# Down products accumulated in PSUM as chains, weight loads tied to matmuls, input rows read once, in a one-core decoder step

## The chip, the cores and the metric

The kernel runs on one core of one Trainium2 chip. The core has TensorE (PE; its weight loads are listed apart as PEld), VectorE (DVE), ScalarE (ACT), GpSimd (POOL) and SyncE (SP), which here only issues DMA transfers. PSUM, the matmuls' output memory, has 8 banks. The metric is the device time of one execution in microseconds (us).

## The reference

One layer of a decoder over 1024 prompt rows and 8 x 8 sample rows, 1088 tokens in all, in float32. The part that the change touches is its end:

```python
mixed = jax.nn.sigmoid(g_a) * branch_a + jax.nn.sigmoid(g_b) * branch_b
h = x + jnp.einsum('btd,de->bte', mixed, w_o)
z = jnp.einsum('btd,df->btf', rms_norm(h, ln2), w_up)
return h + jnp.einsum('btf,fd->btd', jnp.square(jax.nn.relu(z)), w_down)
```

The model width is 1024 and z is 4096 wide. Ahead of it come the input projection, a causal pooling branch and three groups of dilated attention, which make `mixed`, and updated caches are part of the output.

## The kernel before

Everything is transposed: tokens lie along the free axis, channels on the 128 partitions. The 1088 tokens are ordered in four residues of 272 (`Q`); a half (`H`) is two of these, 544 tokens. Each float32 operand of a matmul is split into a high and a low part by one ScalarE copy and one VectorE subtraction (`split`, `put`, lines 113, 1382), and each product is three matmuls (high x high, high x low, low x high).

TensorE's order is the order of the program text. The instructions of the other engines, and of SP's transfer queue, are put in order by a planner that simulates the program; each engine and queue then works strictly in its order. `behind_pe` (line 172) makes an instruction wait for a given matmul; without an argument it takes the last matmul traced by the helpers that keep `last_mm`.

**w_o (lines 1335 to 1355).** For each half `j` of the tokens and each of four weight panels `d`, the panel is read in four 256 KB pieces (three raw buffers, L120) and split (L114, L115). The input rows `xr` of two channel blocks, all 1088 tokens, are read in each of the eight rounds (L1339), into two buffers. VectorE adds them to the product (L1348), giving h: `y[j][kk]`, which is stored (L1349) and squared for the second norm. The norm of half 0 is worked out during half 1, that of half 1 (`norm_sums(1)`, `norm_spread(1)`) after the first two Up products; from it `make_versions` (line 1407) makes the differences of quarters of the normed input.

**Up and Down** are each done with seven products of quarter blocks in place of eight (Strassen's scheme in Winograd's form), in 16 groups. A step is one product for one group: 24 matmuls. `step` puts preparation, matmuls, what follows (`post`), and a load in a list, and `run` (line 1467) emits it: at step n first the loads of steps up to n + 8, then the preparations up to n + 2, then the matmuls, the post, and one of the `later` actions. Preparation splits a weight into one of five places; `raw_tile` has two buffers.

*Up* (`group`, line 1517): P1 is copied out of its PSUM tile by ScalarE (L1532) and P2 is then accumulated onto the same tile. For the first five groups (`FIRST`) P1 and P2 come first, ten steps, while the other operands are made; their results go through the single buffers e1 and e2 (`park`) to memory and are read back (`back`, L1554). The quarters of weights for these ten steps are `raw_uf` (L1497). Afterwards come P5, P6, P7, P3, P4 for these groups, then all seven for the others. Each group's squared results and their sums are stored as seven blocks `z_d` (L1515).

*Down* (`down_stage`, line 1690) has seven stages, in the order P2, P4, P1, P5, P6, P7, P3; a stage is 16 steps, which accumulate into four PSUM tiles of two banks each, all of PSUM. A step loads 256 KB of w_down and 272 KB of z into a half of a raw buffer, or the weight into one of 32 `kept` tiles that later stages use. At a stage's end `post_down` (line 1659) reads the four tiles out: by VectorE, adding onto h rows `hs` or onto `running` (P2, P4, P6), by ScalarE into `running` or `parked` (P1, P5, P7), and by VectorE into the output rows (P3). 24 adds onto `hs` and 8 output row halves are spread over the following steps, one action a step. The h rows are read back in the first stage (L1705).

GpSimd issues 44 transfers that move the caches from input to output (line 1763). Each waits for one of a list of marks, ScalarE splits all along the program.

## Time and profile before

| | us |
|---|---|
| median of 3 runs (1495.24 to 1497.19) | 1496.16 |
| profiled execution | 1495.8 |
| its span, first to last instruction | 1494.0 |
| TensorE busy in it | 1442.5 |
| mean granted TensorE clock | 0.986 |

A row of the timeline gives start, length, engine, line of the kernel, operation, output<-inputs, shape and count; in brackets, how long the engine had stood and what ended that. A row of waits gives total time, times, and the longest. A row of a stretch gives its length, the busy time (and count) of PE, PEld, DVE, ACT and POOL, the granted clock of TensorE as a share of full speed, the mean busy share of the 16 DMA engines, and GB/s. Tile names are the program's: ph is a w_o product, pz an Up product, pd a Down product, places and apart hold split weights.

### The profile page before, as it was taken

To read this page: it belongs to the slowest core of one execution; us is meant where nothing else is said; L and a number is where in the kernel's file an instruction comes from. 1 tells how busy PE (TensorE), PEld (TensorE's weight loads), DVE (VectorE), ACT (ScalarE), POOL (GpSimd) and SP (SyncE) were. 2 spreads that over 40 slices of the span, in tenths; PEclk is the share of its full clock that TensorE was granted. 3 is DMA by queue.
4 is the path that set the end of the run, shared out by engine and by line. 5 is a ranking of instruction groups with operands and counts; after the bars stand their busy time and mean duration, and the time that the engine had idled before them with its cause. 6 is when DMAs were issued, how large, how long until landed. Compare 5 with 4: busy or idle time off the path is not lost. (4 is left out here: it accounts for less than half of the span.)

```text
span 1494.0 us, 28199 instructions
## 1 busy us (share of the span) xinstructions
PE 1442.5 (97%) x10765; PEld 1386.0 (93%) x10765; DVE 899.7 (60%) x1704; ACT 702.0 (47%) x1884; POOL 204.4 (14%) x245
## 2 busy tenths in 40 slices
PE   9999999999999999998998989999999799999988
PEld 8988877888899999998997989999999799999888
DVE  7665674866755444244578766665655345784865
ACT  8566755877533232123435434544454344443342
POOL 1711255556300000010000000000000000000000
PEclk9999999999999999999998999999999899999999
DMA  6312888553545432379757766565668944655664
GB/s 202 110 46 78 229 202 202 169 134 94 148 129 181 136 126 97 113 216 320 263 188 226 249 222 211 186 193 197 208 205 322 352 158 151 224 189 185 204 219 160
DMA packets 164276, 277.91 MB, mean 186 GB/s; under 512 B 32615, under 2 KB 86189, under 8 KB 162414
## 3 DMA queue, kind: packets, MB, share of 16 engines
q1 hardware_dynamic: 158030, 225.79, 47.5%
q0 software_dynamic: 6112, 50.33, 10.6%
q8 instruction: 84, 1.38, 0.4%
q14 instruction: 50, 0.41, 0.1%
HBM read 215.74 MB, written 103.98 MB: 214 GB/s over the span
## 5 line engine op out<-in xcount | busy, mean ns | idle before, releaser
L1741 PE MATMUL pd<-places 128*128 128x272 f32 x2688 | 340.8, 289 | 16.5 <-ACT places L1384 8.4
L1741 PEld LDWEIGHTS pd<-places 128*128 128x128 f32 x2688 | 338.3, 190 | 19.0 <-ACT places L1384 11.1
L1763 POOL DMA_DIRECT2D out_kv_sample_dram<-in_cache_kv_dram x44 | 21.9, 497 | 944.7 <-ACT places L1384 494.9
L1384 ACT ACTIVATE places<-raw_d 128x544 fp32r<-128x544 f32 (+1 forms) x160 | 99.1, 641 | 98.7 <-PE pd L1741 26.0
L1385 DVE TENSOR_TENSOR places<-raw_d,places 128x544 fp32r<-128x544 f32 (+1 forms) x160 | 109.7, 711 | 32.5 <-ACT places L1384 32.2
L1454 PE MATMUL pz<-act,places 128*128 128x272 f32 x912 | 119.5, 289 | 2.8 <-ACT e L1532 2.8
L1454 PEld LDWEIGHTS pz<-act,places 128*128 128x128 f32 x912 | 116.5, 188 | 3.3 <-ACT e L1532 3.2
L184 PE MATMUL ph<-act,places 128*128 128x272 f32 x768 | 99.5, 292 | 5.1 <-ACT places L114 5.1
L184 PEld LDWEIGHTS ph<-act,places 128*128 128x128 f32 x768 | 98.5, 191 | 5.6 <-ACT places L114 5.6
L184 PE MATMUL pga<-act,places 128*128 128x384 f32 (+1 forms) x576 | 100.2, 332 | 0.2 <-ACT places L114 0.2
L184 PE MATMUL pgb<-act,places 128*128 128x384 f32 (+1 forms) x576 | 97.9, 327 | 0.0
L184 PEld LDWEIGHTS pga<-act,places 128*128 128x128 f32 x576 | 96.3, 190 | 1.2 <-issue 0.6
L184 PEld LDWEIGHTS pgb<-act,places 128*128 128x128 f32 x576 | 95.4, 188 | 0.0
L1454 PE MATMUL pz<-act,apart 128*128 128x272 f32 x624 | 85.9, 297 | 6.6 <-ACT e L1532 6.6
L1454 PEld LDWEIGHTS pz<-act,apart 128*128 128x128 f32 x624 | 83.5, 196 | 7.1 <-ACT e L1532 7.0
L1384 ACT ACTIVATE places<-kept 128x512 fp32r<-128x512 f32 x64 | 40.5, 632 | 104.5 <-PE pd L1741 87.4
L1385 DVE TENSOR_TENSOR places<-kept,places 128x512 fp32r<-128x512 f32 x64 | 44.1, 689 | 65.1 <-ACT places L1384 65.0
L600 POOL TENSOR_TENSOR mr<-ms,mhalf 128x4 f32<-128x4 f32 (+2 forms) x39 | 51.9, 1332 | 106.6 <-DVE ms L599 106.4
L1454 PE MATMUL pz<-places 128*128 128x272 f32 x432 | 58.9, 295 | 4.1 <-DVE t L1591 4.1
L184 PE MATMUL pqk<-places,act 128*128 128x512 f32 x240 | 61.0, 403 | 1.0 <-ACT qk L605 1.0
L1454 PEld LDWEIGHTS pz<-places 128*128 128x128 f32 x432 | 57.4, 196 | 4.3 <-issue 4.3
L184 PEld LDWEIGHTS pqk<-places,act 128*128 128x128 f32 x240 | 44.6, 192 | 11.1 <-ACT qk L605 1.2
(382 smaller groups left out, 2657.0 us busy)
## 6 DMA issues: line engine op xcount, KB each, us to landing
out_kv_sample_dram<-in_cache_kv_dram POOLq DMA_DIRECT2D x36, 960.0 KB, 6.2
raw_d<-z_d SPq DMA_DIRECT2D x112, 272.0 KB
z_d<-t SPq DMA_DIRECT2D x86, 272.0 KB
raw_u<-in_w_up_dram SPq DMA_DIRECT2D x64, 256.0 KB
raw_d<-in_w_down_dram SPq DMA_DIRECT2D x64, 256.0 KB
raw_qkv<-in_w_in_dram SPq DMA_DIRECT2D x36, 256.0 KB
xr<-in_xT_dram SPq DMA_DIRECT2D x8, 1088.0 KB
pck<-in_cache_kv_dram SPq DMA_DIRECT2D x32, 256.0 KB
```

What stands on the lines that cost most here:

```text
L184: last_mm[0] = t_.matmul(out, lhs(a, k), rhs(b, k), start=(j == 0), stop=(j == len(terms) - 1))
L600: g_.tensor_tensor(r[:n, :H], ms[:n, :H], mhalf[:n, :H], op=ALU.pow)
L1384: ins = s_.activation(view(t[:, 0]), src, AF.Copy)
L1385: v_.tensor_tensor(view(t[:, 1]), src, view(t[:, 0]).bitcast(F32), op=ALU.subtract)
L1454: t_.matmul(x[:, c, :Q], A[:, a, k * P:(k + 1) * P], Bv(b, k, c), start=(first and n == 0), stop=(n == len(terms) - 1), skip_group_check=n ...
L1741: t_.matmul(q["x"][t][:, c, :Q], A[:, a, t * P:(t + 1) * P], Z[:, b, c * Q:(c + 1) * Q], start=(f == 0 and n == 0), stop=(f == NG - 1 and ...
L1763: ins = g_.dma_start(d, a)
```

## The change

Six things are changed.

- Input rows: `xr` is read only for half 0. ScalarE copies the rows of half 1 into `y[1]`, and in half 1 VectorE adds the product onto them.
- Loads: a step's load is now emitted `lead` steps ahead of it (7 in Up, 6 for the first ten steps, 4 for the first panel of an early group and in Down, never below step 0) and by `behind_pe` waits for the last matmul before that point. The reloads of an early group move from the load to the preparation of P5.
- The first groups' results: e1 and e2 serve every third group, the others use the two buffers t1, t2 each.
- Down's order is P2, P1, P6, P7, P4, P5, P3. P6, P7 and P4 accumulate in PSUM onto P1, and P3 onto P5; P2, P1 and P5 start anew. The weight sums change with it: one block is now read once where it was read twice, another three times instead of once, 16 loads more in all. The h rows are read in the third stage.
- After each stage but the last, ScalarE copies the four tiles into `park_a` or `park_b`; 16 VectorE adds and 8 row halves follow.
- The cache transfers get no mark in Down's first two stages and twice as many in P5.

```diff
@@ -1335,8 +1335,9 @@
     for j in range(2):
         for d in range(4):
             wt = by_k(panel(i["w_o"][d], f"o{j}{d}"))
-            xr = rr(hq_p, [P, 2, TOK], F32, name=f"xr{j}{d}", tag="xr", bufs=2)
-            dma(xr, i["xT"][:, 2 * d:2 * d + 2])
+            if j == 0:
+                xr = rr(hq_p, [P, 2, TOK], F32, name=f"xr{d}", tag="xr", bufs=2)
+                dma(xr, i["xT"][:, 2 * d:2 * d + 2])
             for m in range(2):
                 kk = 2 * d + m
                 po = xtile(f"ph{kk}_{j}")
@@ -1345,7 +1346,11 @@
                     gemm(po[:, c, :Q], KD, lambda s, k: wt[:, s, k, m * P:(m + 1) * P], lambda s, k: act[s][k][:, cs])
                     if todo:
                         todo.pop(0)()
-                v_.tensor_tensor(two(y[j][kk]), xs_of(po), by_token(xr[:, m, :], j), op=ALU.add)
+                if j == 0:
+                    v_.tensor_tensor(two(y[0][kk]), xs_of(po), by_token(xr[:, m, :], 0), op=ALU.add)
+                    s_.copy(two(y[1][kk]), by_token(xr[:, m, :], 1))
+                else:
+                    v_.tensor_tensor(two(y[1][kk]), xs_of(po), two(y[1][kk]), op=ALU.add)
                 dma_st(h_d[kk][:, half(j)], y[j][kk])
                 if kk == 0:
                     s_.activation(sqa[j], y[j][kk], AF.Square)
@@ -1366,7 +1371,7 @@
...
-                t_.matmul(x[:, c, :Q], A[:, a, k * P:(k + 1) * P], Bv(b, k, c),
-                          start=(first and n == 0), stop=(n == len(terms) - 1), skip_group_check=not first)
...
+                last_mm[0] = t_.matmul(x[:, c, :Q], A[:, a, k * P:(k + 1) * P], Bv(b, k, c),
+                                       start=(first and n == 0), stop=(n == len(terms) - 1), skip_group_check=not first)
...
+    def step(prep, mm, post, load=None, lead=7):
+        if load:
+            loads.setdefault(max(0, len(queue) - lead), []).append(load)
+        queue.append((prep, mm, post))
...
+    def run(ahead=3):
+        n_prep = 0
...
-            while n_load < min(len(queue), n + load_ahead):
-                if queue[n_load][0]:
-                    queue[n_load][0]()
-                n_load += 1
+            for load in loads.get(n, ()):
+                load()
...
     def load_panel(f):
         raws[f] = raw_tile(f"u{f}")
         for a in range(0, 2048, 512):
-            dma(raws[f][:, a:a + 512], i["w_up"][f][:, a:a + 512])
+            behind_pe(dma(raws[f][:, a:a + 512], i["w_up"][f][:, a:a + 512]))
...
     def load_first(f):
         if f % 2 == 0:
             raws["first", f // 2] = raw_tile(f"uf{f}")
         for a in range(2):
-            dma(first_quarter(f, a).rearrange("p (k n) -> p k n", k=4),
-                i["w_up"][f].rearrange("p (k n) -> p k n", k=8)[:, 4 * a:4 * a + 4, :P])
+            behind_pe(dma(first_quarter(f, a).rearrange("p (k n) -> p k n", k=4),
+                          i["w_up"][f].rearrange("p (k n) -> p k n", k=8)[:, 4 * a:4 * a + 4, :P]))
...
-    def park(n, name):
-        return rr(up, [P, H], F32, name=f"e{n}_{name}", tag=f"e{n}", bufs=1)
+    def park(n, f):
+        if f % 3:
+            return temp(n, f"e{f}")
+        return rr(up, [P, H], F32, name=f"e{n}_{f}", tag=f"e{n}", bufs=1)
...
             step(lambda: weights(0, 0), lambda A: products(xt(), A, B["11"], True), first_post,
-                 (lambda: load_first(f)) if early else (lambda: load_panel(f)))
+                 (lambda: load_first(f)) if early else (lambda: load_panel(f)), 6 if early else 7)
...
         def back():
-            load_panel(f)
             for n, src in ((1, p_d[f]), (2, z_d[f, :, 0, :])):
                 firsts[f][n - 1] = temp(n, f"again{f}")
                 dma(firsts[f][n - 1], src)
@@ -1563,8 +1569,12 @@
                 q["x5"] = q["x"]
                 q["s5"] = temp(4, f)
                 s_.copy(two(q["s5"]), xs_of(q["x"]))
-            step(lambda: summed(1, quarter(f, 1, 0), quarter(f, 1, 1), ALU.add),
-                 lambda A: products(xt(), A, B["T1"], True), post, back if early else None)
+            def prep():
+                if early:
+                    back()
+                return summed(1, quarter(f, 1, 0), quarter(f, 1, 1), ALU.add)
+            step(prep, lambda A: products(xt(), A, B["T1"], True), post,
+                 (lambda: load_panel(f)) if early else None, 7 if f else 4)
...
         for t in range(4):
             x = xs_of(xs[t])
-            v, w = parked[:, t], running[:, t]
-            if p in (2, 4):
-                kt = t if p == 2 else 4 + t
-                v_.tensor_tensor(two(hs[kt][:, half(0)]), two(hs[kt][:, half(0)]), x, op=ALU.add)
+            a, b = park_a[:, t], park_b[:, t]
+            if p == 2:
+                s_.copy(two(a), x)
             if p == 1:
-                s_.copy(two(w), x)
-                later.append(adds(t, 0, w))
+                s_.copy(two(b), x)
+                later.append(lambda a=a, b=b: v_.tensor_tensor(a, a, b, op=ALU.add))
+            if p == 6:
+                s_.copy(two(b), x)
+                later.extend((adds(t, 0, a), adds(t, 1, b)))
+            if p == 7:
+                s_.copy(two(a), x)
+                later.append(adds(4 + t, 1, a))
+            if p == 4:
+                s_.copy(two(b), x)
+                new_row(4 + t)
+                later.append(lambda t=t, b=b: row_half(4 + t, 0, two(b)))
             if p == 5:
-                s_.copy(two(v), x)
-                later.extend((adds(t, 1, v), adds(4 + t, 1, v)))
-            if p == 6:
-                v_.tensor_tensor(two(w), two(w), x, op=ALU.add)
-                later.extend((adds(4 + t, 0, w), adds(t, 1, w), adds(4 + t, 1, w)))
-            if p == 7:
-                s_.copy(two(v), x)
-                new_row(4 + t)
-                later.append(lambda t=t, v=v: row_half(4 + t, 0, two(v)))
-                later.append(lambda t=t, v=v: (row_half(4 + t, 1, two(v)), row_done(4 + t)))
+                s_.copy(two(a), x)
+                later.append(lambda t=t, a=a: (row_half(4 + t, 1, two(a)), row_done(4 + t)))
             if p == 3:
                 row_half(t, 1, x)
                 row_done(t)
-        if p == 7:
+        if p == 5:
             for t in range(4):
                 later.append(lambda t=t: (new_row(t), s_.copy(by_token(rows[t], 0), two(hs[t][:, half(0)]))))
...
         def load(f):
-            if p == 2 and f >= KD:
-                kt = f - KD
-                hs[kt] = op.tile([P, TOK], F32, name=f"hs{kt}")
-                dma(hs[kt], h_d[kt])
+            if p == 6 and f % 2 == 0:
+                hs[f // 2] = op.tile([P, TOK], F32, name=f"hs{f // 2}")
+                behind_pe(dma(hs[f // 2], h_d[f // 2]))
             if f % 2 == 0:
                 q[f] = raw_tile(f"d{p}_{f}")
             w, z = parts(f)
-            if p == 4:
-                dma(kept[1, f], of(f, 1, 1))
-            elif p == 1:
-                dma(kept[2, f], of(f, 0, 0))
-            elif p != 6:
-                dma(w, of(f, *((1, 0) if p in (5, 7) else (0, 1))))
-            dma(z, z_d[f, :, ZI[p], :])
+            block = {2: (0, 1), 1: (1, 0), 7: (1, 1), 4: (1, 1), 3: (0, 1)}.get(p)
+            if block:
+                behind_pe(dma(w, of(f, *block)))
+            behind_pe(dma(z, z_d[f, :, ZI[p], :]))
+            if p == 1:
+                behind_pe(dma(kept[1, f], of(f, 0, 0)))
+            n = f + {2: -4, 1: 12}.get(p, NG)
+            if 0 <= n < NG:
+                behind_pe(dma(kept[2, n], of(n, 1, 1)))
...
         def prep(f):
             w, z = parts(f)
-            if p in (4, 1):
-                w = kept[1 if p == 4 else 2, f]
-            elif p in (5, 6):
-                k1 = kept[1, f]
-                if p == 5:
-                    v_.tensor_tensor(k1, w, k1, op=ALU.add)
-                else:
-                    v_.tensor_tensor(k1, k1, kept[2, f], op=ALU.subtract)
+            k1, k2 = kept.get((2, f)), kept.get((1, f))
+            if p == 1:
+                v_.tensor_tensor(k1, w, k1, op=ALU.add)
+                w = k2
+            elif p == 6:
+                v_.tensor_tensor(k2, k1, k2, op=ALU.subtract)
+                w = k2
+            elif p == 5:
                 w = k1
-            elif p == 7:
-                v_.tensor_tensor(w, kept[2, f], w, op=ALU.subtract)
-            elif p == 3:
-                v_.tensor_tensor(w, w, kept[1, f], op=ALU.subtract)
+            elif p in (7, 3):
+                v_.tensor_tensor(w, w, k2, op=ALU.subtract)
             return put_down(w, z)
         def mm(f, AZ):
             A, Z = AZ
-            if f == 0:
-                q["x"] = [xtile(f"pd{p}_{t}") for t in range(4)]
+            fresh = p in (2, 1, 5)
+            if f == 0 and fresh:
+                chain[:] = [xtile(f"pd{p}_{t}") for t in range(4)]
+            q["x"] = chain
             for t in range(4):
                 for c in range(2):
                     for n, (a, b) in enumerate(PASSES):
-                        t_.matmul(q["x"][t][:, c, :Q], A[:, a, t * P:(t + 1) * P], Z[:, b, c * Q:(c + 1) * Q],
-                                  start=(f == 0 and n == 0), stop=(f == NG - 1 and n == 2))
+                        last_mm[0] = t_.matmul(chain[t][:, c, :Q], A[:, a, t * P:(t + 1) * P], Z[:, b, c * Q:(c + 1) * Q],
+                                               start=(fresh and f == 0 and n == 0), stop=(f == NG - 1 and n == 2),
+                                               skip_group_check=not fresh)
         for f in range(NG):
             step(lambda f=f: prep(f), lambda AZ, f=f: mm(f, AZ),
-                 (lambda: post_down(p, q["x"])) if f == NG - 1 else (lambda: None), lambda f=f: load(f))
-
-    for p in (2, 4, 1, 5, 6, 7, 3):
+                 (lambda: post_down(p, q["x"])) if f == NG - 1 else (lambda: None), lambda f=f: load(f), 4)
+
+    chain = []
+    for p in (2, 1, 6, 7, 4, 5, 3):
         down_stage(p)
...
     n_up = 7 * NG
     late = [t for t in throttle[13:-8] for _ in range(4)] + [t for t in throttle[-8:] for _ in range(2)]
-    late += marks_f[:n_up] + marks_f[n_up + 24:-20:2]
+    down = [marks_f[n_up + 32 * n:n_up + 32 * n + 32:2] for n in range(7)]
+    late += marks_f[:n_up] + [m for n in (2, 3, 4, 5, 5, 6) for m in down[n][:16 - 10 * (n == 6)]]
```

22 lines of the change are left out of this document (9 added, 13 removed).

## The prediction

> **What bounds the kernel now.** I read the page first (engine shares), then who TensorE waited for, then TensorE's timeline around each pause, then the loads and the queue that caused it. Of the page:
> ```profile
> span 1494.0 us, 28199 instructions
> PE 1442.5 (97%) x10765; PEld 1386.0 (93%) x10765; DVE 899.7 (60%) x1704; ACT 702.0 (47%) x1884; POOL 204.4 (14%) x245
> raw_d<-z_d SPq DMA_DIRECT2D x112, 272.0 KB
> raw_d<-in_w_down_dram SPq DMA_DIRECT2D x64, 256.0 KB
> ```
> TensorE is busy 97%, and the change removes no matmul. So all that can be won is pauses, and the slow clock behind them. The waits of TensorE from 665 to 1130 us (w_o and the Up products), and in Down, which follows:
> ```profile
> PE pz L1454 <- ACT e L1532: 9.3, 4, 4.7
> PE ph L184 <- ACT places L114: 5.1, 1, 5.1
> PE pz L1454 <- DVE t L1591: 4.1, 1, 4.1
> ```
> ```profile
> L1741 PE MATMUL pd<-places 128*128 128x272 f32 x2688 | 340.8, 289 | 16.5 <-ACT places L1384 8.4
> ```
> That is 18.5 us before Down (columns: total, times, longest) and, by the page's group of Down's matmuls, 16.5 us idle in Down. The timeline says when (start, length; in brackets the pause before):
> ```profile
> 693.46 34.55 PE L184 MATMUL ph<-act,places 128*128 128x272 f32 x258 [5.13 <-ACT places L114]
> 782.36 4.81 PE L1454 MATMUL pz<-act,apart 128*128 128x272 f32 x24 [1.91 <-ACT e L1532]
> 827.37 3.15 PE L1454 MATMUL pz<-t,places 128*128 128x272 f32 x24
> 883.33 5.73 PE L1454 MATMUL pz<-places 128*128 128x272 f32 x24 [4.07 <-DVE t L1591]
> 1189.55 192.69 PE L1741 MATMUL pd<-places 128*128 128x272 f32 x1535 [0.37 <-DVE places L1385]
> 1439.95 10.10 PE L1741 MATMUL pd<-places 128*128 128x272 f32 x79 [2.11 <-ACT parked L1677]
> ```
> Unbroken, 1535 matmuls take 192.69 us: 125.5 ns each, 3.01 us for a step of 24. After a pause 24 took 5.73 instead of 3.15: the granted clock. In its windows (length, busy PE, PEld, DVE, ACT, POOL, then PEclk, DMA share, GB/s):
> ```profile
> 690.87:697.70 6.83, 4.24 (x18) 4.25 (x19) 2.04 (x3) 1.89 (x3) 0.00 (x0) 0.50 0.97 358
> 783.05:786.46 3.41, 3.41 (x17) 3.41 (x16) 3.24 (x5) 1.27 (x2) 0.00 (x0) 0.50 0.89 281
> 800.12:806.95 6.83, 4.49 (x20) 4.49 (x21) 5.26 (x6) 2.31 (x4) 0.00 (x0) 0.50 0.75 203
> 882.04:888.87 6.83, 5.54 (x24) 5.58 (x25) 6.71 (x11) 4.64 (x8) 0.00 (x0) 0.50 0.30 102
> 1175.59:1182.41 6.82, 4.18 (x17) 3.87 (x18) 2.75 (x4) 2.57 (x4) 0.49 (x1) 0.50 1.19 441
> 1189.24:1192.65 3.41, 3.10 (x13) 3.10 (x14) 2.66 (x5) 1.22 (x3) 0.00 (x0) 0.50 0.37 111
> ```
> Half of the busy PE time in each is lost: 2.1, 1.7, 2.2, 2.8, 2.1 and 1.6 us.
>
> **Down: the stages in a new order.** The pauses behind ScalarE's L1384, 8.4 us, lie where the last two of these windows are, and are late loads. The program's own queue (SP), where the kept weights are issued ahead of need:
> ```profile
> 1149.30 5.75 SPq L1710 DMA_DIRECT2D kept<-in_w_down_dram  x6
> ...
> 1174.08 5.60 SPq L1712 DMA_DIRECT2D kept<-in_w_down_dram  x9
> ```
> The chain of waits shows what that burst does to the other loads, against one outside it:
> ```profile
> 871.21 9.84 DMA raw_u<-in_w_up_dram
> ...
> 1142.57 10.71 DMA raw_d<-in_w_down_dram
> ...
> 1378.41 3.86 DMA raw_d<-in_w_down_dram
> ```
> All 32 kept loads (16 for each of two stages) go out in 31 us, for steps up to 48 steps away, and a needed load takes 10.7 us instead of 3.9. The change ties each load to the step four before its use, and moves the eight h loads to the third stage. Gone by that: 8.4 us and 2.1 + 1.6 of clock, 12.1 us.
>
> The new traffic must fit. A step of the first stage (P2) carries 256 + 272 KB, from its fifth step on 256 more: 784 KB in 3.01 us, 267 GB/s. P1 starts with four steps of 1040 KB, 354 GB/s, and goes on at 267. Sixteen weight loads are added in all (P4 reads its block again). The burst window moved 441 GB/s, and the cache shifts are taken out of these two stages, so I cost the bytes at nothing; the cover is the four steps. Four steps are 12.05 us. From it go 0.45 for the issue and the preparation, whose parts are (median durations in ns between slashes):
> ```profile
> L1384 ACT ACTIVATE places<-raw_d x160: 615/640/672, 1120.5 to 1476.7; 128x544 fp32r<-128x544 f32 x112, 128x512 fp32r<-128x512 f32 x48
> L1385 DVE TENSOR_TENSOR places<-raw_d,places x160: 678/718/769, 1121.7 to 1479.0; 128x544 fp32r<-128x544 f32 x112, 128x512 fp32r<-128x512 f32 x48
> ```
> 0.69 for a weight sum (L1731 below), 2 x 0.64, 0.72: 2.7 us. A load may take 8.9 us; outside the burst it takes 3.9. If this cover goes, the price is in the slower rival.
>
> The other 8.1 us, at 1384 and about 1440, are crowding of VectorE at stage ends. There, evacuations and sums of rows queue ahead of or behind weight preparation:
> ```profile
> 1383.50 0.71 DVE L1674 TENSOR_TENSOR running<-running,pd 128x544 f32<-128x544 f32 x1
> ...
> 1439.61 0.69 DVE L1731 TENSOR_TENSOR raw_d<-raw_d,kept 128x512 f32<-128x512 f32 x1 [0.96 <-DMA raw_d<-in_w_down_dram]
> ...
> 1441.46 6.05 DVE L1651 TENSOR_TENSOR row<-hs,parked 128x544 f32<-128x544 f32 x6
> ```
> With chains, six of seven stages end in four ScalarE copies, and VectorE keeps 16 adds and 8 row halves where it had 12 evacuations, 24 adds and 8 row halves: 20 x 0.71 us less. A ScalarE copy takes 0.60:
> ```profile
> L1671 ACT COPY parked<-pd x4: 594/604/619, 1332.5 to 1334.9; 128x544 f32<-128x544 f32 x4
> ```
> Accumulating onto a tile just copied waits for that copy, as reusing its place did. The same shape stands at 1332 (P5 to P6) inside the unbroken 192.69 us, so I price the wait at nothing. ScalarE has 4 x 0.60 + 2 x 0.64 = 3.7 us in a step of 3.0 there, so up to 0.7 at each of six ends, 4 us, if it has no work ahead. So 4 of the 8.1 go, and of the whole of Down 16 (bounds: 10, where a stage end costs 1 us more, and 20.2, all of it with the clock).
>
> **Up, the first ten steps.** Four pauses wait for the copy into e, a single buffer whose store must land first; each chain P1 to P2 also waits for the copy itself. Three buffers instead of one leave the copy alone: 0.60 us and 0.3 of hand-over, my estimate (half the copy), 3.6 us in all. Of 9.3 + 1.7 + 2.2 some 9.6 could go. But behind the second norm stands VectorE's chain that makes the other operands, and its end follows that norm, not these steps:
> ```profile
> 777.47 5.62 DVE L1327 SCALAR_TENSOR_TENSOR y<-y,cols,bc 128x544 f32<-128x544 f32 x8 [0.27 <-PE bc L1324]
> ...
> 818.94 1.28 DVE L115 TENSOR_TENSOR t<-y,t 128x1088 fp32r<-128x1088 f32 x1
> ```
> It ends 42.8 us after it starts, and the fourth step of the first full group reads it, at 827.37, 49.9 after. If the chain keeps its length the steps can win 7.1, not 9.6. I take 7 (bounds 4, were the chain 3 us longer, and 10).
>
> Against it stands **a new pause** where w_o ends. The loads of the first Up weights (raw_uf) lie within w_o now; as the first steps have no earlier step, they are tied to w_o's last matmul. TensorE then waits through issue 0.45, landing, ScalarE 0.64, VectorE 0.72. The transfers just before are few (the last two numbers are DMA share and GB/s):
> ```profile
> 760.00:770.00 10.00, 10.00 (x82) 10.00 (x82) 3.53 (x4) 0.87 (x2) 0.00 (x0) 1.00 0.20 77
> ```
> So I take the 3.86 above: 5.7 us, and the halved clock as at 882, 2.8: 8.5 lost. Bounds 6.5 (less clock) and 14.5 (landing as at 871).
>
> A rule has a cheaper landing: the Trainium skill's "DMA: Bandwidth & Descriptors", section "Anatomy of one DMA — SWDGE (gpsimd) path", fits 2.0 us plus bytes over 436 GB/s; as an estimate that is 2.6 us for 256 KB, this pause 4.4 and the sum 1.3 us lower. The Trainium skill's fit is for another issuing engine, and none of the three landings quoted here is that short.
>
> **The pause at 883** (4.07 + 2.8): VectorE, which works in order, stood at a weight sum whose panel took the 9.84 us above to land, with L1591 behind it:
> ```profile
> 881.13 0.69 DVE L1558 TENSOR_TENSOR sm<-raw_u 128x512 f32<-128x512 f32 x1 [8.25 <-DMA raw_u<-in_w_up_dram]
> ```
> Panels tied seven steps ahead keep the same two buffers, so they hardly come earlier; but the planner now sees them no earlier than TensorE allows. I take 4 of 6.9 (bounds 0 and 6.9).
>
> **What else moves.** The two reloads of an early group (272 KB each) are issued two steps before its first step now, and first read after the second: four steps, 12 us, cover a landing of 3.9 to 9.8, so nothing; were they late, VectorE's add after P6 would stand. A load that waits for TensorE in SP's queue holds the stores of z behind it, at most about a step; their single buffers are written again a group (seven steps, 21 us) later, so nothing. Outside the pause at w_o's end, the queue's waits end before the step they belong to. GpSimd's cache shifts get 86 marks in Down for 90 and skip the first two stages: nothing, as no pause waits for them.
>
> **w_o: rows read once.** Four loads of 1088 KB go from the second half, where no pause lies (693.46, 34.55 us unbroken): nothing. Eight ScalarE copies come into the first half. A like copy, and the engines of that half (ACT is the fifth number):
> ```profile
> L1686 ACT COPY row<-hs x4: 1173/1194/1215, 1448.9 to 1454.2; 128x544 f32<-128x544 f32 x4
> ```
> ```profile
> 665.00:722.00 57.00, 51.87 (x398) 51.65 (x397) 26.75 (x37) 17.91 (x29) 0.51 (x1) 0.94 0.90 313
> ```
> That is 8 x 1.19 = 9.5 us on an engine busy 17.91 of 57: hidden. If one stood in the queue waiting for its rows, it would hold the weight splits behind it; that is the lower bound below. The pause at 693 is another matter:
> ```profile
> 663.19 1.01 SPq L1497 DMA_DIRECT2D raw_uf<-in_w_up_dram  x2
> ...
> 668.60 4.12 SPq L1497 DMA_DIRECT2D raw_uf<-in_w_up_dram  x2
> 672.77 0.98 SPq L1339 DMA_DIRECT2D xr<-in_xT_dram  x2
> ```
> Eight raw_uf loads (2.1 MB, 5.9 us at 358 GB/s) stand ahead of w_o's own, one holding the queue 4.1 us. They go. Of 5.13 + 2.1 I take 5; bounds 7.2 and minus 4.8 (four copies of 1.19 in front of the splits).
>
> **Sum**: 16 + 7 - 8.5 + 4 + 5 = 23.5 us off the profiled execution's 1495.8 (span 1494.0; it is 0.4 under the median 1496.16): **1472 us**. With the terms off by half their bounds, not all to one side, 1462 to 1482.
>
> **The rivals.**
> *Down gains, Up does not.* The new pause costs 14.5, the 883 and 693 pauses stay, the ten steps give 4, Down 16: 5.5 off, 1490; with the middle value of the pause 1484. For it: the landings of 9.84 and 10.71. Against: the 77 GB/s before 770.
> *Nothing moves.* The pauses in Down come from stage ends as such, and one at each chain link takes their place: six of 2.7 us for the 16.5. 1492 to 1499. Against it: the unbroken 192.69 us over three stage ends.
> *Slower: the lead of four steps is too short.* In P2 and P1 each pair of buffers comes late if loads take 10.7 us as at 1142: 1.8 us each, 16 pairs, 29 us, and halved clock up to 1.7 behind each, 27 more: 1501 to 1528. It decides from a landing of 10.4 us (16 x 1.5 eats the 23.5). For it: 267 to 354 GB/s asked for. Against: spread issue, no shifts there.
> On the clock a rule differs: the Trainium skill's page "TensorE: Matmul & The Clock Gate", section "Why this matters for your kernels", lets gaps up to some 3 us pass. Here the 1.91 us pause at 782 was followed by 0.50; by the rule this rival would stay at 1501.
>
> **How the numbers follow.** Forecast 0.62, Down alone 0.20, nothing 0.04, slower 0.14. Within 0.2% (3 us, about what a measurement of this kernel tells from no change) only the third: faster 0.82, same 0.04, slower 0.14. The range runs from 1460 to 1490, over the first two.
>
> **What would show it.** Right: no pause over 1 us between matmuls at Down's stage ends, kept loads spread evenly, none at 690; a pause of 5 to 6 us before the first Up product; about 0.9 us behind each early P1. Wrong: ScalarE standing at an xr copy in w_o; weight preparation in P1 ending at DMA each step; TensorE waiting for t (T4) in the first full group.

## The result and the profile after

The changed kernel takes 1476.71 us (median of 4 runs, 1471.04 to 1480.75) against 1496.18 for the kernel before on the same chip: ratio 0.9867, with a 95% interval of 0.9829 to 0.9906. The prediction was 1472 us in a range of 1460 to 1490. The profiled execution is the slowest of the four, 1480.75 us, and its granted clock was 0.991 where it was 0.986 before. Of the page of after, the span, the engines' busy times, and the group of Down's matmuls (busy time and mean ns, then the idle time ahead of them and what ended most of it):

```profile
span 1479.0 us, 28245 instructions
PE 1440.9 (97%) x10765; PEld 1384.2 (94%) x10765; DVE 888.5 (60%) x1684; ACT 721.0 (49%) x1904; POOL 204.2 (14%) x245
L1753 PE MATMUL pd<-places 128*128 128x272 f32 x2688 | 336.6, 287 | 3.5 <-ACT park_b L1680 2.0
```

Down's matmuls had 16.5 us of idle time before and have 3.5 now; their busy time fell by 4.2 us, of which the halved clock that followed two of the old pauses makes 3.7 (2.1 and 1.6). What TensorE waits for from w_o to the end, in after (total, times, longest):

```profile
PE rth L1311 <- DVE sqa L1360: 4.6, 1, 4.6
PE pz L1459 <- ACT t_e L1539: 4.2, 3, 2.8
PE pz L1459 <- ACT places L1389: 3.7, 1, 3.7
PE pz L1459 <- DVE t L1591: 2.8, 3, 1.9
PE pd L1753 <- ACT park_b L1680: 2.0, 1, 2.0
```

Five kinds of pause stand in place of the old ones: one in w_o ahead of the second norm's sums (rth), which the prediction doesn't have; the pause at the start of Up (L1389), which it has; pauses behind the copies of P1 (t_e); pauses behind VectorE's L1591; and one at a stage end of Down (L1680). The timeline of TensorE in after tells when, and what the matmuls behind each pause took:

```profile
728.84 1.87 PE L1311 MATMUL rth<-ones,sqa 128*128 128x1 f32 x10 [4.63 <-DVE sqa L1360]
730.64 8.56 PE L184 MATMUL ph<-act,places 128*128 128x272 f32 x48
...
776.79 4.81 PE L1459 MATMUL pz<-act,places 128*128 128x272 f32 x24 [3.72 <-ACT places L1389]
...
814.32 7.82 PE L1459 MATMUL pz<-act,places 128*128 128x272 f32 x48 [2.80 <-ACT t_e L1539]
...
848.15 4.81 PE L1459 MATMUL pz<-t,places 128*128 128x272 f32 x24 [1.94 <-DVE t L1591]
...
1279.79 143.87 PE L1753 MATMUL pd<-places 128*128 128x272 f32 x1152 [1.99 <-ACT park_b L1680]
```

Set side by side from the first matmuls of each part (us, one profiled execution of each):

| part | before | after | difference | predicted |
|---|---|---|---|---|
| to the first w_o product | 663.0 | 666.0 | +3.0 | 0 |
| w_o, first to last product | 105.7 | 106.8 | +1.1 | -5 |
| last w_o to first Up product | 0.1 | 4.0 | +3.9 | +8.5, clock included |
| first ten steps, to P5 of group 0 | 46.5 | 42.2 | -4.3 | -7 |
| rest of Up | 314.5 | 312.9 | -1.6 | -4 |
| Down | 357.2 | 339.9 | -17.3 | -16 |
| behind the last product | 7.0 | 7.3 | +0.3 | 0 |

The differences make the 15.0 us between the spans. The first row says little of the change: the same kernel once more (again, below) has 662.6 there, and the kernels below lie between 661.6 and 668.4. The clock lost behind the 3.72 us pause (24 matmuls in 4.81 us instead of 3.15) stands in the row of the ten steps.

### The profile page after: what moved, and what is told of

Read it like the earlier page. It is cut to its first block, busy times and chain, and to the rows that moved or that the text cites. A ratio compares the mean times of both kernels' runs of the same rounds, so it can differ in the third digit from the quotient of the medians.

```text
span 1479.0 us, 28245 instructions
## 1 busy us (share of the span) xinstructions
PE 1440.9 (97%) x10765; PEld 1384.2 (94%) x10765; DVE 888.5 (60%) x1684; ACT 721.0 (49%) x1904; POOL 204.2 (14%) x245
## 5 line engine op out<-in xcount | busy, mean ns | idle before, releaser
L1753 PE MATMUL pd<-places 128*128 128x272 f32 x2688 | 336.6, 287 | 3.5 <-ACT park_b L1680 2.0
L1389 ACT ACTIVATE places<-raw_d 128x544 fp32r<-128x544 f32 (+1 forms) x176 | 111.0, 647 | 164.4 <-DMA raw_d<-z_d 73.0
L1390 DVE TENSOR_TENSOR places<-raw_d,places 128x544 fp32r<-128x544 f32 (+1 forms) x176 | 122.3, 711 | 94.1 <-ACT places L1389 91.9
L1459 PE MATMUL pz<-act,places 128*128 128x272 f32 x912 | 122.6, 294 | 7.8 <-ACT places L1389 3.7
L1459 PEld LDWEIGHTS pz<-act,places 128*128 128x128 f32 x912 | 119.5, 193 | 8.6 <-ACT t_e L1539 4.0
L1459 PE MATMUL pz<-act,apart 128*128 128x272 f32 x624 | 82.5, 290 | 2.0 <-ACT e L1539 0.8
L1459 PEld LDWEIGHTS pz<-act,apart 128*128 128x128 f32 x624 | 79.9, 188 | 2.7 <-ACT e L1539 1.1
L805 POOL TENSOR_TENSOR pck<-pck,qs 128x256 f32<-128x256 f32 x64 | 47.6, 774 | 43.3 <-DMA pck<-in_cache_kv_dram 20.0
L306 PE MATMUL a<-act,places 128*128 128x384 f32 (+1 forms) x288 | 51.0, 333 | 1.4 <-ACT act L284 1.4
```

Of the source, the lines that this page charges most:

```text
L306: last_mm[0] = t_.matmul(pts[m][:, :n], wt[:, a, kk, m * P:(m + 1) * P], act4[b][kk][:, :, part4(c)], start=(p == 0 and kk == 0), stop=(p ...
L805: behind_pe(g_.tensor_tensor(t[:, n], t[:, n], qs[:, :256], op=ALU.mult))
L1389: ins = s_.activation(view(t[:, 0]), src, AF.Copy)
L1390: v_.tensor_tensor(view(t[:, 1]), src, view(t[:, 0]).bitcast(F32), op=ALU.subtract)
L1459: last_mm[0] = t_.matmul(x[:, c, :Q], A[:, a, k * P:(k + 1) * P], Bv(b, k, c), start=(first and n == 0), stop=(n == len(terms) - 1), skip_ ...
L1753: last_mm[0] = t_.matmul(chain[t][:, c, :Q], A[:, a, t * P:(t + 1) * P], Z[:, b, c * Q:(c + 1) * Q], start=(fresh and f == 0 and n == 0), ...
```

## The experiments

Each kernel was compared with the kernel before on the same chip. The same parts in the profiled execution of each:

| kernel | w_o | to Up | ten steps | rest of Up | Down | median us | ratio, 95% interval |
|---|---|---|---|---|---|---|---|
| again | 102.8 | 3.9 | 41.6 | 312.8 | 341.3 | 1477.58 | 0.9873 (0.9847 to 0.9900) |
| before_rows | 105.6 | 0.1 | 43.7 | 314.1 | 358.2 | 1498.38 | 1.0011 (0.9995 to 1.0027) |
| before_ties | 105.1 | 0.1 | 43.8 | 313.8 | 347.7 | 1484.35 | 0.9929 (0.9903 to 0.9954) |
| chains_untied | 102.8 | 3.9 | 40.3 | 311.8 | 348.8 | 1480.40 | 0.9897 (0.9872 to 0.9922) |
| one_e | 102.8 | 3.9 | 41.9 | 313.1 | 339.7 | 1476.24 | 0.9869 (0.9844 to 0.9893) |
| marks90 | 98.5 | 4.0 | 39.7 | 316.2 | 346.9 | 1479.06 | 0.9887 (0.9865 to 0.9910) |
| first_tie | 100.9 | 0.1 | 38.4 | 313.9 | 341.7 | 1471.85 | 0.9837 (0.9811 to 0.9862) |
| both | 99.7 | 0.1 | 42.3 | 316.0 | 349.0 | 1469.67 | 0.9837 (0.9803 to 0.9872) |
| mix | 99.2 | 0.1 | 41.9 | 313.8 | 339.9 | 1469.15 | 0.9824 (0.9802 to 0.9846) |
| before_marks86 | 104.9 | 0.1 | 40.3 | 310.7 | 358.7 | 1487.59 | 0.9944 (0.9928 to 0.9959) |
| clear_wo | 99.0 | 0.1 | 36.4 | 314.3 | 338.8 | 1461.87 | 0.9769 (0.9754 to 0.9785) |
| clear_one_e | 98.5 | 0.1 | 37.6 | 308.0 | 342.0 | 1457.98 | 0.9743 (0.9717 to 0.9770) |

How far one execution may be trusted is seen in the ten steps of before, before_rows and before_ties, which have the same Up: 46.5, 43.7, 43.8. A difference of under 3 us there needs more than one trace.

**again: the change once more, unchanged.**

> The changed kernel once more, to see what differs between its executions (1471 to 1481 us). Theory: most of the spread is one pause of TensorE at about 728 us, before the first sums of the second norm, with the halved clock behind it (4.63 + 2.3 us in the trace at hand), which depends on how late a w_o piece lands; so median 1473 to 1480, and a faster execution shows this pause shorter. Rival: the spread is the clock alone (windows of half clock in the attention part), and the pause at 728 stays 4 to 5 us in each trace.

It took 1477.58 us (6 runs, 1470.61 to 1480.78). The profiled execution took 1473.92, and in it the pause in w_o is a third as long. Of again, TensorE's timeline:

```profile
722.90 1.18 PE L1311 MATMUL rth<-ones,sqa 128*128 128x1 f32 x10 [1.39 <-DVE sqa L1360]
724.01 7.78 PE L184 MATMUL ph<-act,places 128*128 128x272 f32 x48
```

w_o took 102.8 us in it and 106.8 in after. So that pause is there in both, with a size that changes from one execution to the next, and these 4.0 us are much of the 6.8 between the two profiled times; 3.4 more lie ahead of w_o. The theory held.

**The pause in w_o, and the cache transfers.** In after, the queue's, ScalarE's and VectorE's rows ahead of it (POOL issues a cache transfer, the page gives 960 KB for it and a median of 6.3 us to landing):

```profile
715.41 0.49 POOL L1778 DMA_DIRECT2D out_kv_sample_dram<-in_cache_kv_dram  x1 [17.06 <-ACT places L114]
716.38 7.28 SPq L120 DMA_DIRECT2D raw_o<-in_w_o_dram  x3
726.70 0.63 ACT L114 ACTIVATE places<-raw_o 128x512 fp32r<-128x512 f32 x1 [8.39 <-DMA raw_o<-in_w_o_dram]
727.24 0.64 ACT L1359 ACTIVATE hq<-y 128x544 f32<-128x544 f32 x1
727.97 0.72 DVE L1360 TENSOR_TENSOR sqa<-sqa,hq 128x544 f32<-128x544 f32 x1
```

In before the transfer came later:

```profile
726.19 0.49 POOL L1763 DMA_DIRECT2D out_kv_sample_dram<-in_cache_kv_dram  x1 [25.95 <-ACT places L114]
```

In after it is issued 1 us ahead of three weight pieces of w_o. ScalarE stands 8.39 us at the split (L114) of a piece that is late; the square of a finished row (L1359) stands behind that split in its order; VectorE's sum (L1360) needs the square, and the second norm's product needs the sum. Why did the transfer move? The 44 transfers are spread evenly over the list of marks, and the list is four marks shorter, so every transfer takes an earlier mark. **marks90** gives the list its old length:

```diff
-    late += marks_f[:n_up] + [m for n in (2, 3, 4, 5, 5, 6) for m in down[n][:16 - 10 * (n == 6)]]
+    late += marks_f[:n_up] + [m for n in (2, 3, 4, 5, 5, 6) for m in down[n][:16 - 6 * (n == 6)]]
```

> The changed kernel with 90 marks for the cache transfers in Down in place of 86, so that all earlier transfers stand at the marks of the kernel before. Theory: the 86 marks moved a 1 MB cache transfer from 726 to 715 us, into the second half of w_o, where it held up a weight piece, the split behind it and so the sums of the norm. With 90 the pause at 728 goes: 5 to 7 us faster than the changed kernel, 1468 to 1473. Rival: the pause comes from ScalarE's copies of the input rows or from the new order of its queue; then it stays and the time is within 2 us of the changed kernel.

The pause in w_o is gone and w_o took 98.5 us, 7.2 less than in before. But the whole took 1479.06 us, no less than the change: Down lost 5 to 7 us, at stage ends. Of marks90, TensorE at one of them, and GpSimd and ScalarE ahead of it:

```profile
1369.05 69.22 PE L1753 MATMUL pd<-places 128*128 128x272 f32 x529 [2.83 <-ACT park_b L1686]
```
```profile
1358.46 0.49 POOL L1778 DMA_DIRECT2D out_kv_sample_dram<-in_cache_kv_dram  x1 [14.44 <-ACT places L1389]
1361.08 0.49 POOL L1778 DMA_DIRECT2D out_kv_sample_dram<-in_cache_kv_dram  x1 [2.13 <-ACT places L1389]
1367.32 0.66 ACT L1389 ACTIVATE places<-raw_d 128x544 fp32r<-128x544 f32 x1 [5.99 <-DMA raw_d<-z_d]
```

Two transfers 2.6 us apart, a z load that lets ScalarE stand 5.99 us, and the copies of the stage's end behind that split. The chains made ScalarE the engine that ends a stage, so a late load there now holds TensorE through it. That the two transfers made this load late is read from the one trace. The theory on w_o held and its expectation of the total did not.

**first_tie: the pause at w_o's end.** The first four groups' loads are tied to the matmul before w_o's last panel:

```diff
+            if (j, d) == (1, 3):
+                w_o_mm = last_mm[0]
...
-                          i["w_up"][f].rearrange("p (k n) -> p k n", k=8)[:, 4 * a:4 * a + 4, :P]))
+                          i["w_up"][f].rearrange("p (k n) -> p k n", k=8)[:, 4 * a:4 * a + 4, :P]), w_o_mm if f < 4 else None)
```

> The changed kernel with the loads of the first four early groups tied to the w_o matmul before the last weight panel (12 us earlier) in place of the last w_o matmul. Theory: the pause before the first Up product (3.72 us and 1.6 of halved clock) goes and nothing takes its place, 5 us faster than the changed kernel: 1470 to 1473. Rival: the chain of VectorE behind the second norm sets the end of this part, and the steps only wait later for their operands; then at most 2 us faster, 1475 to 1478.

The pause is gone (last w_o product at 766.8, first Up product at 767.0), and 1471.85 us is 5.7 under again on the same chip, as expected. **both** has this and the 90 marks:

> Both edits in one: 90 marks, and the first loads tied 12 us earlier. If both theories hold the gains add, 10 to 12 us faster than the changed kernel: 1464 to 1467. If the chain behind the second norm is the limit, or the pause at 728 is of another cause, 1469 to 1477.

1469.67 us (6 runs, 1465.51 to 1484.6), above the 1464 to 1467 that two added gains would give. Its profiled execution is the slowest of the six, 15 us above the median; Down took 349.0 us in it, with pauses of 3.2 and 2.3 at stage ends. So in this execution, as in marks90, the transfers' new places cost in Down what their old places had cost in w_o; how much of it is in the median, one trace doesn't show.

**mix** has the early tie too, but moves back only the first ten transfers and leaves Down's as the change has them; **before_marks86** takes four marks from the kernel before, and nothing else.

```diff
-        tc.add_manual_dep(ins.ins, late[n * len(late) // len(shifts)].ins.name,
+        tc.add_manual_dep(ins.ins, late[n * (len(late) + 4 * (n < 10)) // len(shifts)].ins.name,
```

> The change with the loads of the first four early groups tied one panel earlier, as before, and of the marks only those of the first ten cache transfers put back to the places they have with 90 marks; Down keeps its 86. Theory (the w_o pause belongs to the 1 MB transfer moved ahead, the new pauses of the 90 marks belong to the transfers moved in Down): no pause before the second norm's sums, none over 1 us at the start of Up, w_o under 103 us, Down 339 to 342, 1466 to 1469 us. Rival (the pauses wander whatever the marks): 1470 to 1474, with a pause of over 2 us in w_o or at Down's stage ends.

w_o 99.2 us with no pause, Down 339.9, as the theory has it; but a pause of 4.66 us behind a copy of P1 stood in the ten steps of the profiled execution, so "none over 1 us at the start of Up" failed. 1469.15 us, at the upper end of what was expected; its interval overlaps that of first_tie.

```diff
-    late += marks_f[:n_up] + marks_f[n_up + 24:-20:2]
+    late += marks_f[:n_up] + marks_f[n_up + 24:-28:2]
```

> The kernel before with 86 marks in Down for 90, by leaving out the last four; nothing else. Theory (four marks fewer move the 1 MB transfer of w_o's second half ahead, before a needed weight piece): it is issued about 715 us for 726, TensorE pauses 1 to 5 us before the second norm's sums, 1497 to 1502 us. Rival (in the change, other parts made that pause; the marks alone do nothing): no pause there, 1494 to 1497.

Both expectations failed: the transfer is issued at 715.14, as the theory has it, but no pause follows, as the rival has it; and the kernel is 9 us faster than before (0.9944, 0.9928 to 0.9959), which neither has. The trace of before_marks86 shows why the pause isn't there:

```profile
715.14 0.49 POOL L1763 DMA_DIRECT2D out_kv_sample_dram<-in_cache_kv_dram  x1 [17.29 <-ACT places L114]
...
720.42 0.66 ACT L1354 ACTIVATE hq<-y 128x544 f32<-128x544 f32 x1 [1.85 <-DVE y L1348]
...
721.48 1.28 ACT L114 ACTIVATE places<-raw_o 128x512 fp32r<-128x512 f32 x2 [0.40 <-DMA raw_o<-in_w_o_dram]
```

Here the square stands ahead of the split in ScalarE's order. So it takes both: the transfer ahead of the pieces, and the split ahead of the square; the change brought both. marks90 has the second without the first: split at 717.10, square at 717.64, the transfer only at 719.10, and no pause. The five traces of the change with the transfer between 713 and 717 us (after, again, one_e, chains_untied, first_tie) all have the pause, of 1.3 to 4.6 us; the five in which it comes later or not at all (marks90, both, mix, clear_wo, clear_one_e) have none. The gain of before_marks86 lies mostly in Up (ten steps 3.4 to 6.2 us, the rest 3.1 to 3.8, by which of before, before_rows and before_ties it is held against). Of the waits of before_marks86 from 640 to 1494 us, the row on e:

```profile
PE pz L1454 <- ACT e L1532: 5.1, 4, 2.3
```

They were 9.3 in before, and the pause of 4.07 behind L1591 isn't there. So a good part of what the change was to bring in Up can come from moving the cache transfers alone. How the change's gain in the ten steps divides between these and the other parts, the runs don't settle: marks90 (the change with 90 marks) has 39.7 us, before_marks86 (nothing but the marks) 40.3, and both at once, in the change, 42.2 and 41.6 behind the pause at w_o's end.

**clear_wo: no cache transfer in w_o and in the ten steps**, with the early tie of first_tie. The list loses the marks of these stretches:

```diff
-    late = [t for t in throttle[13:-8] for _ in range(4)] + [t for t in throttle[-8:] for _ in range(2)]
+    late = [t for t in throttle[13:-8] for _ in range(4)]
...
-    late += marks_f[:n_up] + [m for n in (2, 3, 4, 5, 5, 6) for m in down[n][:16 - 10 * (n == 6)]]
+    late += marks_f[10:n_up] + [m for n in (2, 3, 4, 5, 5, 6) for m in down[n][:16 - 10 * (n == 6)]]
```

> The change with the same early tie, and with no cache transfer marked in w_o or in the first ten Up steps; all 44 lie closer in what is left. Theory (a cache transfer costs only where it delays a weight piece with little lead): w_o 98 to 101 us with no pause, the first ten steps under 38 us, 1465 to 1469 us. Rival (the transfers, moved closer together, collide in attention, the rest of Up and Down): 1471 us or more with pauses of over 2 us there.

1461.87 us, 3 under the expected range. w_o 99.0, the ten steps 36.4, Down 338.8. One long pause was left, and the trace of clear_wo says what it is:

```profile
823.47 0.72 DVE L1624 TENSOR_TENSOR t<-t_again,t 128x544 f32<-128x544 f32 x1
...
831.07 0.72 DVE L1584 TENSOR_TENSOR t_again<-t_again,pz 128x544 f32<-128x544 f32 x1 [5.08 <-DMA t_again<-p_d]
831.83 0.72 DVE L1593 TENSOR_TENSOR t<-t_again,pz 128x544 f32<-128x544 f32 x1
```
```profile
824.22 0.32 SPq L1562 DMA_DIRECT2D t_again<-p_d  x1
```
```profile
832.60 5.03 PE L1461 MATMUL pz<-t,places 128*128 128x272 f32 x24 [5.04 <-DVE t L1593]
```

VectorE's add after P6 waits for the reload of P1 (p_d) of the second early group. That reload is issued at 824.22, just when VectorE has read the first group's tile for the last time (823.47 and 0.72). The two buffers of t1 are handed out in turn, in the program's order: the fifth group's result takes one after the first group's reload has taken the other, so the second group's reload gets that of the first. In after the same row stands at the pause of 1.94 us:

```profile
846.63 0.72 DVE L1582 TENSOR_TENSOR t_again<-t_again,pz 128x544 f32<-128x544 f32 x1 [2.56 <-DMA t_again<-p_d]
```

**one_e and clear_one_e: the buffers.** one_e is the change with the single buffers e1 and e2 for the first groups' results, as before:

```diff
     def park(n, f):
-        if f % 3:
-            return temp(n, f"e{f}")
         return rr(up, [P, H], F32, name=f"e{n}_{f}", tag=f"e{n}", bufs=1)
```

> The changed kernel with the single buffers e1 and e2 for all five early groups again. Theory: the pauses behind their stores come back, 5 us in the first ten Up steps and 2 of clock, 1480 to 1486. Rival (VectorE's chain behind the second norm sets the end of this part anyway): within 2 us of the changed kernel, 1474 to 1479.

1476.24 us, what the change has. With a single buffer, its TensorE timeline has:

```profile
787.12 3.29 PE L1459 MATMUL pz<-act,apart 128*128 128x272 f32 x24 [0.72 <-ACT e L1537]
...
795.77 7.66 PE L1459 MATMUL pz<-act,places 128*128 128x272 f32 x48 [2.35 <-ACT e L1537]
```

Three of its four pauses behind e are 0.70 to 0.72 us: the copy alone, where before had up to 4.7. In the fourth, of 2.35, ScalarE had stood 1.52 us until a store of e (p_d) had landed. So the stores do hold a single buffer, but in this trace only once. In before they were the cause of the longest pause. Of before, SP and ScalarE:

```profile
788.52 4.71 SPq L1491 DMA_DIRECT2D raw_u<-in_w_up_dram  x4
793.34 0.35 SPq L1515 DMA_DIRECT2D z_d<-e  x1
...
800.59 0.62 ACT L1538 ACTIVATE e<-pz 128x544 f32<-128x544 f32 x1 [7.13 <-DMA z_d<-e]
```

ScalarE had written e2 by 789.42, but its store is issued at 793.34, behind four loads of a weight panel that take SP's queue 4.71 us. ScalarE stands 7.13 us for the store, and the copy of P1 behind it in its order lets TensorE stand 4.65. before_rows and before_ties show the same (5.23 and 4.97 us at this store, TensorE 5.03 and 4.49), before_marks86 has 2.79 at it and TensorE 0.70. In one_e the loads of these panels (raw_u) are issued from 800.45 on, and no store there is waited for over 1.52 us. So the wait can be taken away without more buffers.

The pause behind L1591 isn't in one_e: the t1 and t2 buffers that the change lends to the first groups' results are those into which the reloads go. Its rest of Up is no shorter even so, for pauses of 0.99 and 2.27 us stand there that after doesn't have. clear_one_e takes the loan out of clear_wo:

> As with the early tie and no cache transfer in w_o and the first ten Up steps, and in addition e1 and e2 single again, so that the first groups' results take no buffer of t1 and t2. Theory (the pause of 5.04 us at 832 there, as that of 1.94 at 848 in the change, is the second early group's reload of P1, which finds no free buffer until VectorE has read the first group's): the reload is issued at least 8 us before its use, that pause is gone, 1455 to 1459 us. Rival (the single buffers bring back 1 to 3 us of pauses behind e in the ten steps, or the pause comes from the transfers near 824 us): no gain, 1460 to 1464 us.

1457.98 us (5 runs, 1453.79 to 1459.9). The second group's reload is issued at 780.79 for 824.22, and of the waits of TensorE, from 640 to 1494 us, this is what is left:

```profile
PE pz L1461 <- ACT e L1539: 4.0, 4, 1.9
PE pd L1753 <- ACT park_a L1675: 1.9, 1, 1.9
PE pd L1753 <- ACT park_a L1690: 1.7, 1, 1.7
PE pd L1753 <- ACT park_b L1680: 0.6, 1, 0.6
PE pz L1461 <- DVE t L1591: 0.5, 1, 0.5
```

The rest of Up took 308.0 us for 314.3. The theory held. The medians are 3.9 us apart and the intervals of the two ratios overlap a little, so the trace carries this point more than the times do. It is the fastest kernel of this study, 2.6% under before.

**The two halves of the change in Down.** before_ties is the kernel before with Down's loads emitted four steps ahead and tied, in its old order:

```diff
-                dma(kept[1, f], of(f, 1, 1))
+                behind_pe(dma(kept[1, f], of(f, 1, 1)))
...
-                dma(w, of(f, *((1, 0) if p in (5, 7) else (0, 1))))
-            dma(z, z_d[f, :, ZI[p], :])
+                behind_pe(dma(w, of(f, *((1, 0) if p in (5, 7) else (0, 1)))))
+            behind_pe(dma(z, z_d[f, :, ZI[p], :]))
```

> The kernel before, its order of stages kept; only Down's loads are emitted four steps ahead and tied to the last matmul before that step. Theory (late loads are one half of Down's loss, crowding at stage ends the other): the pauses of 6.15 and 2.23 us and their halved clock go, those at the ends of P6 and P7 stay; Down 343 to 347 us instead of 357, 1483 to 1487 in all. Rival (ties are all of it): Down 340 or less, 1480 or less.

chains_untied is the change without `behind_pe` on Down's loads (the lead of four steps stays):

```diff
-                behind_pe(dma(w, of(f, *block)))
-            behind_pe(dma(z, z_d[f, :, ZI[p], :]))
+                dma(w, of(f, *block))
+            dma(z, z_d[f, :, ZI[p], :])
```

> The changed kernel with Down's loads still emitted four steps ahead, but tied to no matmul. Theory: the planner then issues the loads into the 32 kept tiles and the h rows as early as it can, and they crowd the needed ones as before: pauses of 5 to 10 us in Down's first three stages, 1482 to 1488. Rival (the order of stages and the chains are what helps, the ties add nothing): Down as in the changed kernel, about 340 us, 1474 to 1480.

Down took 357.2 us in before, 347.7 with the ties alone, 348.8 with the rest alone, 339.9 with both: 9.5 and 8.4 for 17.3, so they add, within the 1 us by which Down differs between before and before_rows. The rest is the new order, the chains, ScalarE's copies, the lead and the new marks together; no run parts these. What is left in each is mostly what the other takes away. In before_ties, one late load is left (2.88 us at 1226.51, behind a split whose weight came late), and pauses at stage ends behind VectorE's evacuation:

```profile
1373.25 0.99 PE L1743 MATMUL pd<-places 128*128 128x272 f32 x6 [1.21 <-DVE running L1676]
...
1377.56 48.85 PE L1743 MATMUL pd<-places 128*128 128x272 f32 x378 [2.13 <-DVE running L1676]
```

In chains_untied, late loads in the second stage:

```profile
1183.66 0.59 PE L1753 MATMUL pd<-places 128*128 128x272 f32 x1 [4.43 <-ACT places L1389]
```

before_ties came out as expected but for Down, 0.7 above its range. The total of chains_untied, 1480.40 us, is 1.6 below its expected range, and its longest pause in Down is these 4.43 us, under the 5 to 10 expected.

**before_rows: the rows read once, alone.**

```diff
+                if j == 0:
+                    v_.tensor_tensor(two(y[0][kk]), xs_of(po), by_token(xr[:, m, :], 0), op=ALU.add)
+                    s_.copy(two(y[1][kk]), by_token(xr[:, m, :], 1))
+                else:
+                    v_.tensor_tensor(two(y[1][kk]), xs_of(po), two(y[1][kk]), op=ALU.add)
```

> The kernel before, and only the input rows read once, with ScalarE's copies. Theory: the eight early Up loads cause the 5.13 us pause at 690, so it stays, and no pause comes: 1494 to 1497. Rival one: the 4.5 MB less shorten it, 1488 to 1492. Rival two: the copies stand in ScalarE's queue ahead of weight splits and cost up to 4.8 us: 1498 to 1503.

1498.38 us, 1.0011 (0.9995 to 1.0027): no gain, and no loss clear of noise. The figure lies in rival two's range, but the trace doesn't bear this rival out: ScalarE did stand 7.0 us in all at three of the copies, waiting for their rows, and TensorE has no pause behind them (w_o 105.6 us for 105.7). The pause of before at 693 stays:

```profile
694.81 34.33 PE L184 MATMUL ph<-act,places 128*128 128x272 f32 x258 [5.10 <-ACT places L114]
```

It stands with 4.10 to 5.13 us in the four kernels with the old raw_uf loads (before, before_rows, before_ties, before_marks86). Where these are tied to matmuls near w_o's end, no pause in w_o's first half is over 0.91 us.

## Why the prediction was right, and where not

The total came out 4.7 us above the forecast and well within the range; the signs of the two large terms, Down and the pause at w_o's end, are as forecast. That it came so close is in part luck: of the terms in these traces w_o fell 6.1 short and the two of Up 3.4, while the pause at w_o's end cost 3.1 less than taken and Down brought 1.3 more. Step by step:

- *Down, 16.* Measured 17.3. The split was off: the ties were put at 12.1 and brought 9.5 alone; the chains were put at 4 and brought 8.4 alone, marks moved with them. "No pause over 1 us at Down's stage ends" failed in two of six (1.99 and 1.06 us), neither with a halved clock behind it.
- *A new pause at w_o's end, 8.5.* The mechanism was right, the size too large: 3.72 us and 1.66 of clock (24 matmuls in 4.81 us for 3.15), 5.4 in all; taking it away was worth 5.7. The landing was mis-sized. In after, SP and ScalarE there:

```profile
773.10 0.94 SPq L1502 DMA_DIRECT2D raw_uf<-in_w_up_dram  x2
```
```profile
776.11 0.63 ACT L1389 ACTIVATE places<-raw_uf 128x512 fp32r<-128x512 f32 x1 [1.53 <-DMA raw_uf<-in_w_up_dram]
```

  Two issues take 0.94, so the first is out at 773.57, and ScalarE starts 2.54 later, where 3.86 was taken. And the first matmul waited for ScalarE's high part alone, not for VectorE's 0.72 as well. The Trainium skill's fit in "DMA: Bandwidth & Descriptors", section "Anatomy of one DMA — SWDGE (gpsimd) path", which the prediction set aside, gives 2.6 us for 256 KB as an estimate, and this landing agrees with it. Little else was in flight: 0 GB/s from 770.00 to 773.10.
- *w_o, 5.* This term failed: w_o took 1.1 longer in the profiled execution, and 2.9 less in again, one_e and chains_untied, where the new pause is shorter. The step that it rests on was right (raw_uf gone, no pause at 693). What failed is "GpSimd's cache shifts get 86 marks in Down for 90 …: nothing, as no pause waits for them". The shorter list moved every transfer, and with ScalarE's new order one of them cost 4.63 us and 2.3 of clock (48 matmuls in 8.56 us, which take 6.25 in marks90). With the old list the term is 7.2, the whole of its upper bound. That nothing waits for a transfer was the wrong question: what lands behind it waits.
- *The first ten steps, 7.* 4.3 measured; 6.0 without the clock lost behind the pause ahead of them, and some 2.8 less of each if before_rows or before_ties is taken for before. The cause given, "a single buffer whose store must land first", is right for the longest pause of before (ScalarE's 7.13 us). What failed is the step from there to more buffers: with single buffers the pauses are nearly as short (one_e), since the store then lands in time. Price and limit came nearer: 0.9 us was taken for the copy alone and 0.70 to 0.72 measured; and the longest pause that remained, 2.80 at 814, stands behind VectorE's chain. In after, the copy into t_e comes behind a split that waits for it:

```profile
812.66 1.11 ACT L114 ACTIVATE places<-u 128x1088 fp32r<-128x1088 f32 x1 [1.22 <-DVE u L1425]
813.67 0.59 ACT L1539 COPY t_e<-pz 128x544 f32<-128x544 f32 x1
```

- *The pause at 883, 4 of 6.9.* It went, and a smaller one came at 848: 1.94 and 1.7 of clock, so 3.3 net; the row of the table shows 1.6, and shorter pauses (0.34 to 0.47 us) came too. The step that failed is "The two reloads of an early group …: so nothing". The prediction named what would be late (VectorE's add after P6), and it was; what it missed is that the reloads share their buffers with the results that the change puts there. With neither pause the rest of Up takes 308.0 us for 314.5.
- *Rows read once: nothing.* Right, by before_rows. Of the prediction's signs of being wrong, "ScalarE standing at an xr copy in w_o" did come (3.4 us in three waits in after), and it cost nothing: TensorE ran 450 matmuls over it without a pause (57.02 us from 667.18).
- *The rivals.* The lead of four steps was long enough: no stage of Down waits for weights each step. By the rule that the prediction quotes for the clock (the Trainium skill's "TensorE: Matmul & The Clock Gate", section "Why this matters for your kernels": gaps up to some 3 us pass), 1.94 at 848 should have been free, and it was not.

## What to carry to other kernels

Count a background transfer by what lands behind it, not by who waits for it, and look again at all of them when the list that spaces them changes length. When one pause is taken away, ask what the freed or lent buffers were holding back, and look for the next late thing in the order of the engine that now ends the stage. Parts of a change that each gain the same stretch may not add: undo and do each alone.

## What the hardware showed that was not expected

The halved clock does not follow from the length of a pause alone. In after the pauses of 1.94, 2.80 and 3.72 us were each followed by a stretch of 3.41 us at half clock, the one of 4.63 by 6.83 us. Of after (length, busy PE, PEld, DVE, ACT and POOL, then the granted clock, DMA share and GB/s):

```profile
729.03:735.86 6.83, 6.83 (x33) 6.80 (x33) 2.61 (x7) 2.33 (x4) 1.57 (x2) 0.50 0.35 118
776.81:780.22 3.41, 3.41 (x15) 3.41 (x16) 1.88 (x3) 1.30 (x3) 0.56 (x1) 0.50 0.94 267
814.34:817.75 3.41, 3.41 (x15) 3.41 (x16) 3.41 (x5) 2.20 (x3) 0.00 (x0) 0.50 0.88 338
848.46:851.88 3.42, 3.42 (x17) 3.42 (x16) 3.35 (x6) 1.86 (x3) 0.00 (x0) 0.50 0.34 121
```

But the 1.99 us at 1279 cost no clock (1152 matmuls in 143.87 us, 125 ns each), while 1.39 us in again was followed by 48 matmuls in 7.78 us for 6.25. And of two equal pauses in clear_one_e the first cost none (48 in 6.28) and the second some 1.8 us (786 at 125 ns are 98.2):

```profile
797.72 6.28 PE L1461 MATMUL pz<-act,places 128*128 128x272 f32 x48 [1.85 <-ACT e L1539]
...
1159.08 100.01 PE L1753 MATMUL pd<-places 128*128 128x272 f32 x786 [1.86 <-ACT park_a L1675]
```

From w_o to the last product, the stretches at half clock in before and after last 3.4 us or twice that. The Trainium skill, "TensorE: Matmul & The Clock Gate", section "What's actually happening", describes a free-running window of some 3.4 us; the lengths agree with it.

Where these stretches lie settles the rest. By the clock records of after they start at 729.01, 776.80, 814.35 and 848.48 us: 47.79, 37.55 and 34.13 apart, which is 14, 11 and 10 times 3.413. In each of the 14 traces, all starts and ends of this part lie on one such grid, to 0.002 us; only its offset differs from execution to execution. So a trace can be divided into these windows, and the share of each in which TensorE stood added up, with the products of one column ahead of the norm (rth) counted as standing. Of 3202 windows at full clock, the 47 in which it stood over 55.5% were all followed by one at half clock; of the 3147 in which it stood under 50.5% none was; the eight between went either way.

With this the cases above come out. The 1.94 us at 848 lie in one window (845.07 to 848.48) and fill 57% of it. The 1.99 us at 1279 fall across an edge of the grid at 1278.56, 0.76 and 1.23 us, so neither window is half filled. Of the two equal pauses in clear_one_e, the first falls across the edge at 797.58 and leaves 50% in the window ahead of it, the second lies in one window and fills 54%. And the 1.39 us in again are joined by the 1.1 of rth in the same window. A pause under 1.7 us that stands alone in its window was free in these traces. One of 1.7 to some 3.8 us (twice 55.5% of 3.413, an estimate from these counts) is free or not by where it falls on the grid.
